# One decoder step on one core: pairwise weight sums built in SBUF tiles, with small edits at the head, the sample values, the page units and the tail

## The chip, the core and the metric

The kernel runs on one core of one Trainium2 chip, as one launch. The metric is the device time of one execution in microseconds (us), the median of several runs of the same program. The engines are named as the profile names them: PE (matrix engine; PEld are its weight loads), DVE (vector), ACT (scalar), POOL (general), SP (the queue that issues most transfers). A "q" behind a name (SPq, ACTq) is that engine's instruction queue, which takes its instructions strictly in order: an instruction that waits holds all those behind it.

## What is computed

One inference step of a single decoder layer over 512 prompt tokens and 64 sample tokens (8 sequences of 8), model width 2048. All projections come from one combined weight `w_in`:

```python
z = jnp.einsum('btd,de->bte', h, w_in)             # h = rms_norm(x, norm_in)
qa, ka, va, ga, qi, ki, wi, qb, kb, vb, gb, ab = jnp.split(z, offs, axis=-1)
...
att = dsa_prompt(qa, ka, va, qi, ki, wi)           # top-k of index scores, then softmax attention
att = dsa_sample(qa, ka, va, qi, ki, wi, cache_k, cache_v, cache_idx_k, page_table)
ob, s_fin = gla(qb, kb, vb, la, s0)                # gated linear attention, 4 heads
...
a = att.reshape(B, T, -1) * jax.nn.silu(ga)
bpart = rms_norm(o_b, gla_norm).reshape(B, T, -1).astype(a.dtype) * jax.nn.silu(gb)
xs = xs + jnp.einsum('bte,ed->btd', jnp.concatenate([a, bpart], axis=-1), w_out)
y_sample = rms_norm(xs, norm_f)
```

Eight attention heads of 128 read a paged cache of 1024 past positions for the sample tokens. The outputs are the normalised result for both token sets, and the new keys, values, index keys and linear-attention states.

## The kernel before, in words

Each float32 matrix product is made of three matmuls on rounded parts: a weight tile `w_raw` (128 x 512) is loaded by SP, ACT casts it to a rounded `w_hi` (L196), and the remainder `w_lo` is subtracted on DVE or POOL (L199). `wload` (L188) does this for one weight tile, with 3 buffers of `w_raw` and 5 of each part; `gemm` runs four such tiles per column block of 128. `WOFF` is the priority offset by which the scheduler hoists weight loads ahead of other work. `lo_eng` names the engine of the remainder: POOL during heads 0 to 3, DVE otherwise.

The program runs in stages. At the head, `split_x` (L221) loads the transposed tokens k-slice by k-slice and splits them into `xh` and `xl`, and `first_piece` (L208) splits the first weights. Then come the index projections and `sample_scores`, whose per-sequence key parts are `kch` and `kcl` (L508, L509). Heads 0 to 3 follow (`head`), with projections q and k (each rotated, then cast to `qh`, `kh` on ACT at L630), scores, the gate `ga`, and `head_out`. During them the prompt's top-k runs in the background (`turned`, `far`, `top`). `vgroup` (L649) makes the values of four heads at once; its last lines make the sample rows of the values: copy of one half of an accumulator into the tile `v_smp`, an add of the other half, a scale by the tokens' norm into `vaS`. The tile `v_smp` has the tag `e1`, that is, it shares two buffers with `v_tok`, whose contents go out by transfers.

In heads 4 to 7 and later, `units` reads the paged cache: each unit fetches tiles `kt` or `vt`, multiplies scores (`pS`, 32 output columns at a time), takes the softmax and multiplies by values. `filler` steps the units between the pieces of the gemms, one step of the generator `unit_steps` at a time.

The output projection uses a fast two-by-two scheme: besides the plain blocks of `w_out` it needs four sums of blocks (S1 = block 01 + ..., and so on), for the first half of the rows (p = 0) and for the second (p = 1). Those of p = 0 are added on DVE in tiles `bs` within `units`. Those of p = 1 live in the DRAM tile `spill_t[1]`, which rows of the trace call `st`. `block_parts` (L771) lists 16 pieces of 512 KB. In heads 0 to 2 each of the next weight loads is followed by one transfer `st<-in_wo` on SP (L194: DRAM to DRAM), 16 in all. In heads 2 and 3, each remainder on POOL is followed by one accumulating transfer on POOL's queue (L203): 8 of `st<-in_wo`, then 8 of `st<-st`, DRAM to DRAM.

At the tail the last matmuls (`acc_s`) give the sample rows of the last quarter in two pieces of 256 columns. They are folded (two partition halves of the accumulator and the residual `ysm`), squared and summed (L1584), the root and its reciprocal taken (L1449, L1587), and both halves scaled and stored (L1589 to L1592).

Of the kernel before, what the change touches and what calls it, by code (L numbers as in the profile page):

```python
# [10 lines left out]
F32 = mybir.dt.float32  # L11
# [108 lines left out]
def build(tc, I, O):  # L120
# [64 lines left out]
    started, added = [], []  # L185

    def wload(src, far=0):
        with tc.high_priority(offset=WOFF):  # L188
# [3 lines left out]
            if started:  # L192
                with tc.issue_after(wloads[-1]):
                    sy.dma_start(*started.pop(0))  # L194
# [5 lines left out]
            if lo_eng[0] is po_:  # L200
                if added:
                    with tc.issue_after(getattr(c, "ins", c)):
                        po_.dma_start(*added.pop(0), accum_op=ALU.add)  # L203
# [4 lines left out]
    def first_piece(b, k):  # L208
# [10 lines left out]
        ve.tensor_tensor(out=lo[:, c], in0=raw[:, c], in1=hi[:, c].bitcast(F32), op=ALU.subtract)  # L219

    def split_x(k):  # L221
        if k == 0:
            sy.dma_start(x0[:, : NK + HT], I["x0"][:, : NK + HT])
            sy.dma_start(x0[:, NK + HT :], I["x0"][:, NK + HT :])
            first_piece(0, k)
# [12 lines left out]
        for c, x in parts:  # L238
            ve.scalar_tensor_tensor(out=l[:, c], in0=x, scalar=gn_in[:, k : k + 1], in1=h[:, c].bitcast(F32), op0=ALU.mult, op1=ALU.subtract)
# [106 lines left out]
    po_.memset(vaS[:TS], 0.0)  # L346
# [131 lines left out]
    def sample_scores():  # L478
# [14 lines left out]
        for half in range(2):  # L493
            for grp in range(2):
                for m in range(4):
# [12 lines left out]
                    ve.tensor_tensor(out=kcl[hr], in0=raw, in1=kch[hr].bitcast(F32), op=ALU.subtract)  # L508
                    se.copy(kcl[other], kcl[hr].bitcast(F32))  # L509
# [139 lines left out]
    def vgroup(g, step):  # L649
# [48 lines left out]
        vt = ev.tile([P, 512], F32, name="v_smp", tag="e1", bufs=2)  # L698
        se.copy(vt[TS:], accs[4][:TS])
        ve.tensor_tensor(out=vt[TS:], in0=accs[4][TS:], in1=vt[TS:], op=ALU.add)  # L700
        to = vaS[TS:, cols] if g < 2 else vt[TS:]
        ve.tensor_scalar(out=to, in0=vt[TS:], scalar1=sst[TS:, 4:5], scalar2=None, op0=ALU.mult)
# [68 lines left out]
    def block_parts():  # L771
        first, second = [(0, 0), (0, 1), (1, 1), (1, 0)], [(0, 1), (1, 1), 0, 2]
        for j in range(4):
            for k in range(0, 8, 2):
                block = lambda half, q: I["wo"][2 + q, :, 8 * half + k : 8 * half + k + 2, :]
                more = block(*second[j]) if j < 2 else spill_t[1][:, second[j], k : k + 2, :]
                yield spill_t[1][:, j, k : k + 2, :], block(*first[j]), more

    def head(h, bg, n):
# [7 lines left out]
        if h == 0:  # L787
# [10 lines left out]
            for to, src, _ in block_parts():  # L798
                started.append((to, src))
        if h == 2:  # L800
            assert not started
            for to, _, more in block_parts():
                added.append((to, more))
# [869 lines left out]
```

## Time and profile before

| | us |
|---|---|
| runs | 1203.16, 1198.15, 1203.48; median 1203.16 |
| profiled execution | 1195.22 |
| its span | 1193.3 |
| granted PE clock over the span | 0.998 |
| PE busy in the span | 1179.5 (99%) |
| PEld, DVE, ACT, POOL busy | 1039.7, 727.4, 584.8, 307.2 |
| DMA over the span | 260 MB, 218 GB/s |

The span runs from the first to the last instruction that the profiler records; 1.9 us of the profiled execution lie around it. PE's busy time includes overlapping starts of pipelined matmuls, so what counts below is the time in which PE had no matmul to run: 1193.3 - 1179.5 = 13.8 us. In rows of waits, "A <- B: t, n" says that A stood idle for t us, n times, until B released it. In the chain of waits the columns are start, duration, and what filled that time.

### The profile page before, as it was taken

The page shows a single profiled execution, that of the slowest core. Times are in us where ns is not written, and L with a number is a line of the kernel's source. Part 1 is how long each engine was busy: PE and PEld are TensorE (multiplying, and loading weights), DVE is VectorE, ACT ScalarE, POOL GpSimd, SP SyncE. Part 2 cuts the span into 40 slices and gives each one's busy share as a digit, 9 for nine tenths or more (in the row PEclk, how much of TensorE's full clock was granted, in tenths as well). Part 3 has the DMA queues.
Part 4 walks back from the last instruction along what each step waited for, and adds up shares of the span by engine and source line. Part 5 has one row for each costly group of instructions (what it writes and reads, how often), then busy time and mean ns, then how long its engine had stood idle before and what let it go on. Part 6 is the DMA issues. An engine that isn't in the chain of part 4 may idle for free.

```text
span 1193.3 us, 22985 instructions
## 1 busy us (share of the span) xinstructions
PE 1179.5 (99%) x8383; PEld 1039.7 (87%) x8389; DVE 727.4 (61%) x1347; ACT 584.8 (49%) x1044; POOL 307.2 (26%) x495
## 2 busy tenths in 40 slices
PE   9999999999999999999999999999999999999997
PEld 8999987799999779789998769778899999888886
DVE  6677899699746432565445434434566444657786
ACT  6887564444443332345344435426367533544454
POOL 1225665446631110100112311321041221012100
PEclk9999999999999999999999999999999999999999
DMA  8662233876973999988867675677715377669873
GB/s 291 212 179 95 91 107 108 265 234 160 227 189 92 363 328 373 346 313 304 283 207 244 221 266 202 228 242 227 253 46 179 123 257 240 220 173 234 244 234 116
DMA packets 142419, 259.98 MB, mean 218 GB/s; under 512 B 15633, under 2 KB 38818, under 8 KB 141730
## 3 DMA queue, kind: packets, MB, share of 16 engines
q1 hardware_dynamic: 136370, 243.83, 60.9%
q0 software_dynamic: 4928, 13.11, 6.3%
q10 hardware_dynamic: 1008, 1.57, 0.4%
q8 instruction: 66, 1.08, 0.4%
q14 instruction: 47, 0.39, 0.1%
HBM read 224.62 MB, written 50.48 MB: 231 GB/s over the span
## 4 chain that ended last, share of the span: by engine, by line
PE 82%; DVE 7%; DMA 5%; issue 2%; ACT 2%; SPq 1%; POOL 1%; ACTq 0%; DVEq 0%; POOLq 0%
PE ps_g L249 37%; PE ps_g L254 6%; PE ps_g L662 5%; PE ps_g L664 5%; PE ps_g L663 5%; PE pOs L284 2%; PE acc L1390 2%; PE acc L1389 2%; PE acc L1391 2%; PE pS L284 2%; DMA w_raw<-in_w 2%; DMA y<-in_xp 2%; PE ps_v L658 1%; PE ps_v L659 1%; DVE w_lo L1384 1%
## 5 line engine op out<-in xcount | busy, mean ns | idle before, releaser
L249 PE MATMUL ps_g<-xh,w_hi 128*128 128x288 f32 x1312 | 391.6, 298 | 0.2 <-ACT xh L237 0.2
L249 PE MATMUL ps_g<-xl,w_hi 128*128 128x288 f32 x1312 | 287.6, 296 | 0.0
L249 PE MATMUL ps_g<-xh,w_lo 128*128 128x288 f32 x1312 | 284.5, 296 | 0.6 <-DVE w_lo L219 0.6
L196 ACT CAST w_hi<-w_raw 128x512 fp32r<-128x512 f32 x252 | 154.2, 619 | 250.4 <-PE ps_g L249 94.0
L249 PEld LDWEIGHTS ps_g<-xh,w_hi 128*128 128x128 f32 x1312 | 246.5, 188 | 4.7 <-issue 2.5
L199 DVE TENSOR_TENSOR w_lo<-w_raw,w_hi 128x512 fp32r<-128x512 f32 x188 | 134.9, 723 | 181.2 <-ACT w_hi L196 176.6
L249 PEld LDWEIGHTS ps_g<-xl,w_hi 128*128 128x128 f32 x1312 | 212.3, 188 | 2.3 <-issue 1.2
L249 PEld LDWEIGHTS ps_g<-xh,w_lo 128*128 128x128 f32 x1312 | 211.4, 188 | 1.6 <-DVE w_lo L219 0.8
L199 POOL TENSOR_TENSOR w_lo<-w_raw,w_hi 128x512 fp32r<-128x512 f32 x64 | 86.9, 1359 | 54.9 <-ACT w_hi L196 46.5
L662 PE MATMUL ps_g<-w_hi,xh 128*128 128x512 f32 x256 | 100.7, 395 | 0.0
L664 PE MATMUL ps_g<-w_hi,xl 128*128 128x512 f32 x256 | 100.6, 393 | 0.0
L663 PE MATMUL ps_g<-w_lo,xh 128*128 128x512 f32 x256 | 100.1, 391 | 0.0
L1384 DVE TENSOR_TENSOR w_lo<-w_raw,w_hi 128x1024 fp32r<-128x1024 f32 (+1 forms) x60 | 68.3, 1150 | 42.4 <-ACT w_hi L1382 42.2
L1382 ACT CAST w_hi<-w_raw 128x1024 fp32r<-128x1024 f32 (+1 forms) x60 | 59.4, 994 | 62.5 <-PE acc_s L1394 21.8
L1390 PE MATMUL acc<-w_lo,fh 128*128 128x512 f32 x216 | 84.1, 389 | 0.0
L1391 PE MATMUL acc<-w_hi,fl 128*128 128x512 f32 x216 | 84.1, 389 | 0.0
L1389 PE MATMUL acc<-w_hi,fh 128*128 128x512 f32 x216 | 83.6, 389 | 0.0
L664 PEld LDWEIGHTS ps_g<-w_hi,xl 128*128 128x128 f32 x256 | 48.1, 188 | 10.7 <-issue 0.8
L662 PEld LDWEIGHTS ps_g<-w_hi,xh 128*128 128x128 f32 x256 | 48.0, 188 | 10.0 <-DVE ev_t L622 0.3
L663 PEld LDWEIGHTS ps_g<-w_lo,xh 128*128 128x128 f32 x256 | 48.1, 188 | 9.7
L623 POOL TENSOR_TENSOR ev_sw<-ev_sw,c_s 128x576 f32<-128x576 f32 x16 | 25.3, 1581 | 88.3 <-ACT ev_sw L620 88.2
L1389 PEld LDWEIGHTS acc<-w_hi,fh 128*128 128x128 f32 x216 | 40.5, 188 | 8.4
(394 smaller groups left out, 2089.1 us busy)
## 6 DMA issues: line engine op xcount, KB each, us to landing
w_raw<-in_w SPq DMA_DIRECT2D x188, 256.0 KB, 3.6
kt<-in_ck SPq DMA_DIRECT2D x128, 256.0 KB, 5.1
vt<-in_cv SPq DMA_DIRECT2D x128, 256.0 KB, 5.1
w_raw<-in_wv SPq DMA_DIRECT2D x64, 256.0 KB, 3.3
w_raw<-st SPq DMA_DIRECT2D x32, 512.0 KB, 5.1
w_raw<-in_wo SPq DMA_DIRECT2D x20, 512.0 KB, 6.8
st<-in_wo SPq DMA_DIRECT2D x16, 512.0 KB, 5.0
bs<-in_wo SPq DMA_DIRECT2D x32, 256.0 KB, 5.5
```

The lines of the kernel that those rows point to most:

```text
L196: c = se.copy(hi, raw)
L199: c = lo_eng[0].tensor_tensor(out=lo, in0=raw, in1=hi.bitcast(F32), op=ALU.subtract)
L249: pe.matmul(ps[:, j, :HT], wt, xt[k][:, j * HT : (j + 1) * HT], start=(k == 0 and n in (0, 2)), stop=(k == NK - 1 and n > 3))
L254: m = pe.matmul(ps[:, 0, :TQ], wt[:, c], xt[:, P:T], start=(k == 0 and n == 0), stop=(k == NK - 1 and n == 2))
L662: pe.matmul(accs[i], xh[k][:, c], wh, start=a, stop=False)
L663: pe.matmul(accs[i], xh[k][:, c], wl, start=False, stop=False)
L664: m = pe.matmul(accs[i], xl[k][:, c], wh, start=False, stop=b)
L1382: se.copy(hi, raw)
L1384: ve.tensor_tensor(out=lo, in0=raw, in1=hi.bitcast(F32), op=ALU.subtract)
L1389: pe.matmul(acc, f[0][:, k, c], wh, start=a, stop=False)
L1390: pe.matmul(acc, f[0][:, k, c], wl, start=False, stop=False)
L1391: return pe.matmul(acc, f[1][:, k, c], wh, start=False, stop=b)
```

## The change

Six edits, in the order of the program:

1. Head: `first_piece` returns its subtraction, and for k = 0 the split `xl` on DVE is issued behind the first `w_lo`.
2. `kcl`: its subtraction and copy get a higher priority.
3. Sample values: in `vgroup` 0 and 1 the copy, add and scale are done in place in `vaS`; the tile `v_smp` is left to groups 2 and 3. The clearing of `vaS` moves into `vgroup`.
4. Sums for p = 1: `block_parts` and the two lists go; `block_moves` hangs transfers on the numbered weight loads ("slots") of heads 0 to 3. The pieces are made in four groups of four, at slots 0, 7, 14, 20. A group has an SBUF tile `bt` (128 x 4 x 2 x 512, two buffers). On SP, each of its four pieces is loaded (`bt<-in_wo`, L786) behind one slot's weight load. On POOL, each gets one accumulating transfer behind a slot's remainder: two add a block of `w_out` from DRAM, two add another piece of the same tile (`bt<-bt`, L793). On SP again, each finished piece is stored to `spill_t[1]` (`st<-bt`, L796).
5. Units: in the first four heads' units (hg == 0) two rest steps stand between the first fetch and the first scores, in place of one.
6. Tail: the two partition halves of the last residual are folded earlier over all 512 columns; each of the two pieces then needs two adds in place of three (the first) or two and a copy on ACT (the second); each 256-column piece is squared by itself, and one small DVE instruction adds the first piece's sum to `pre`.

```diff
     SUMS = ((0, 0), (0, 1), (1, 1), (1, 0))
-    started, added = [], []
+    moves, slot = ({}, {}), [None]
+
+    def move(side, lead):
+        for f in moves[side].pop(slot[0], ()):
+            with tc.issue_after(lead):
+                f()
...
-            if started:
-                with tc.issue_after(wloads[-1]):
-                    sy.dma_start(*started.pop(0))
+            move(0, wloads[-1])
...
-            if lo_eng[0] is po_:
-                if added:
-                    with tc.issue_after(getattr(c, "ins", c)):
-                        po_.dma_start(*added.pop(0), accum_op=ALU.add)
+            move(1, getattr(c, "ins", c))
+            if slot[0] is not None:
+                slot[0] += 1
...
-            ve.scalar_tensor_tensor(out=l[:, c], in0=x, scalar=gn_in[:, k : k + 1], in1=h[:, c].bitcast(F32), op0=ALU.mult, op1=ALU.subtract)
+            with tc.issue_after(lo0) if k == 0 else ExitStack():
+                ve.scalar_tensor_tensor(out=l[:, c], in0=x, scalar=gn_in[:, k : k + 1], in1=h[:, c].bitcast(F32), op0=ALU.mult, op1=ALU.subtract)
...
-                    ve.tensor_tensor(out=kcl[hr], in0=raw, in1=kch[hr].bitcast(F32), op=ALU.subtract)
-                    se.copy(kcl[other], kcl[hr].bitcast(F32))
+                    with tc.high_priority(offset=WOFF // 2):
+                        ve.tensor_tensor(out=kcl[hr], in0=raw, in1=kch[hr].bitcast(F32), op=ALU.subtract)
+                        se.copy(kcl[other], kcl[hr].bitcast(F32))
...
-        vt = ev.tile([P, 512], F32, name="v_smp", tag="e1", bufs=2)
-        se.copy(vt[TS:], accs[4][:TS])
-        ve.tensor_tensor(out=vt[TS:], in0=accs[4][TS:], in1=vt[TS:], op=ALU.add)
-        to = vaS[TS:, cols] if g < 2 else vt[TS:]
-        ve.tensor_scalar(out=to, in0=vt[TS:], scalar1=sst[TS:, 4:5], scalar2=None, op0=ALU.mult)
+        if g == 0:
+            po_.memset(vaS[:TS], 0.0)
+        to = vaS[TS:, cols] if g < 2 else ev.tile([P, 512], F32, name="v_smp", tag="e1", bufs=2)[TS:]
+        se.copy(to, accs[4][:TS])
+        ve.tensor_tensor(out=to, in0=accs[4][TS:], in1=to, op=ALU.add)
+        ve.tensor_scalar(out=to, in0=to, scalar1=sst[TS:, 4:5], scalar2=None, op0=ALU.mult)
...
+    def block_moves(pl):
...
+        for g, n in enumerate((0, 7, 14, 20)):
+            k, t = 2 * g, []
+
+            def load(t, k, j):
+                if j == 0:
+                    t.append(pl.tile([P, 4, 2, 512], F32, name="bt", bufs=2))
+                sy.dma_start(t[0][:, j], block(k, j))
...
+            def add(t, k, j):
+                po_.dma_start(t[0][:, j], block(k, j + 1) if j < 2 else t[0][:, (0, 2)[j - 2]], accum_op=ALU.add)
+
+            def keep(t, k, j):
+                sy.dma_start(spill_t[1][:, j, k : k + 2, :], t[0][:, j])
+
+            for j in range(4):
+                at(0, n + j, load, t, k, j)
+                at(1, n + (2, 3, 5, 8)[j], add, t, k, j)
+                at(0, n + (6, 7, 8, 11)[j], keep, t, k, j)
...
         if hg == 0:
-            yield
+            yield from rest(2)
...
-            if s == 0:
-                plus(t[r], a[r2], t[r2])
-                done[ve] = plus(ys, ys, t[r])
-            else:
-                with behind(done, se):
-                    se.copy(yl[r], a[r2])
-                done[ve] = plus(ys, ys, yl[r])
+            done[ve] = plus(ys, a[r2], ys)
+        jk = ev.tile([P, 512], F32, name="yjk", tag="e1", bufs=2)
+        with behind(done, se):
+            done[se] = se.activation(jk[r, :256], ys, AF.Square, accum_out=ysq[r, 4, 3 + s : 4 + s])
+    with behind(done, ve):
+        done[ve] = ve.scalar_tensor_tensor(out=pre[r, 4:5], in0=ysq[r, 4, 3:4], scalar=1.0 / D, in1=pre[r, 4:5], op0=ALU.mult, op1=ALU.add)
     with behind(done, ve):
         scaled(1, 3)
-    jk = ev.tile([P, 512], F32, name="yjk", tag="e1", bufs=2)
-    se.activation(jk[r], y_smp[r, 512:], AF.Square, accum_out=ysq[r, 4, 4:5])
```

What moves on the engines' queues is shown at three places. The first is SP's queue in head 0, behind the values of `vgroup` 0. `w_raw` are weight loads, `st` is the DRAM tile of the sums, `v` the values read back; a name behind "waits" is the semaphore on which the row waits (DMAHW: an earlier transfer of SP or ACT; DMASW: one of POOL; Pool: an instruction of POOL). Before:

```order
L190 DMA w_raw<-in_w 128x512 [waits DMAHW5_49,Pool_49]
L194 DMA st_560<-in_wo 128x1024 [waits DMAHW6_49]
L707 DMA v_3121<-sv_539 128x4x128 [waits DMAHW7_49,DMAHW0_49]
L190 DMA w_raw<-in_w 128x512 [waits Pool_49]
L194 DMA st_560<-in_wo 128x1024 [waits DMAHW1_49]
L190 DMA w_raw<-in_w 128x512 [waits DMAHW2_49,Pool_49]
L194 DMA st_560<-in_wo 128x1024 [waits DMAHW3_49]
L190 DMA w_raw<-in_w 128x512 [waits DMAHW5_49,DMAHW4_49,Pool_49]
L194 DMA st_560<-in_wo 128x1024
```

And now:

```order
L195 DMA w_raw<-in_w 128x512 [waits DMAHW1_49,Pool_49]
L786 DMA bt<-in_wo 128x1024 [waits DMAHW2_49]
L195 DMA w_raw<-in_w 128x512 [waits DMAHW4_49,DMAHW3_49,Pool_49]
L796 DMA st_560<-bt 128x1024 [waits DMASW0_49]
L712 DMA v_3366<-sv_539 128x4x128 [waits DMAHW6_49,DMAHW5_49,DVE_49]
L195 DMA w_raw<-in_w 128x512 [waits DMAHW7_49,Pool_49]
L796 DMA st_560<-bt 128x1024 [waits DMASW1_49]
L195 DMA w_raw<-in_w 128x512 [waits DMAHW1_49,DMAHW0_49,Pool_49]
L195 DMA w_raw<-in_w 128x512 [waits DMAHW3_49,Pool_49]
L796 DMA st_560<-bt 128x1024 [waits DMAHW2_49,DMASW2_49]
L796 DMA st_560<-bt 128x1024 [waits DMASW3_49]
L195 DMA w_raw<-in_w 128x512 [waits DMAHW6_49,DMAHW4_49,Pool_49]
```

Between the weight loads stood loads of pieces into DRAM, which wait only for earlier transfers; now the stores `st<-bt` stand there, and each waits for the accumulating transfer of POOL that finishes its piece. Seven loads `bt<-in_wo` stand ahead of these rows, five of them in a row.

The second place is POOL's queue, with the remainders `w_lo`, the top-k's small copies `turned` and the accumulating transfers. Before, where the first of them stand, behind the 49th remainder on POOL:

```order
L199 TENSOR_TENSOR w_lo<-w_raw,w_hi 128x512
L203 DMA st_560<-in_wo 128x1024
L623 TENSOR_TENSOR ev_sw<-ev_sw,c_s_1535 128x576
L542 COPY turned<-top 128x8
L199 TENSOR_TENSOR w_lo<-w_raw,w_hi 128x512
L203 DMA st_560<-in_wo 128x1024
L542 COPY turned<-top 128x8
L638 COPY qaS<-ev_t_3681 128x64
```

And now the first of them, behind the 38th (`gaS` is head 0's gate):

```order
L546 COPY turned<-top 128x8
L793 DMA bt<-in_wo 128x1024
L202 TENSOR_TENSOR w_lo<-w_raw,w_hi 128x512
L546 COPY turned<-top 128x8
L793 DMA bt<-in_wo 128x1024
L546 COPY turned<-top 128x8
L202 TENSOR_TENSOR w_lo<-w_raw,w_hi 128x512
L546 COPY turned<-top 128x8
L202 TENSOR_TENSOR w_lo<-w_raw,w_hi 128x512
L546 COPY turned<-top 128x8
L727 COPY gaS<-ga 128x64
L793 DMA bt<-bt 128x1024
```

The sixteen accumulating transfers stood behind the 49th to the 64th remainder; now they stand behind the 38th to the 61st, and those of `bt<-bt` among those from `in_wo`, where before all eight of `st<-in_wo` came ahead of all eight of `st<-st`.

The third place is the end of DVE's queue, from the last prompt reciprocal on. Before:

```order
L1453 RECIPROCAL yr<-yr 128x1
L1365 TENSOR_TENSOR y_smp<-acc_s,ysm_12836 64x256
L1365 TENSOR_TENSOR ysm_12836<-acc_s,ysm_12836 64x256
L1365 TENSOR_TENSOR y_smp<-y_smp,ysm_12836 64x256
L1365 TENSOR_TENSOR y_smp<-acc_s,ysm_12836 64x256
L1365 TENSOR_TENSOR y_smp<-y_smp,yl 64x256
L1458 SCALAR_TENSOR_TENSOR y_12830<-y_12830,yr,e_12152 128x512
L1587 RECIPROCAL yr<-yr 64x1 x2
L1591 SCALAR_TENSOR_TENSOR y_smp<-y_smp,yr,nfs 128x512
```

And now:

```order
L1476 RECIPROCAL yr<-yr 128x1
L1388 TENSOR_TENSOR y_smp<-acc_s,ysm_12858 64x256
L1388 TENSOR_TENSOR y_smp<-acc_s,y_smp 64x256
L1388 TENSOR_TENSOR y_smp<-acc_s,ysm_12858 64x256
L1388 TENSOR_TENSOR y_smp<-acc_s,y_smp 64x256
L1602 SCALAR_TENSOR_TENSOR pre<-ysq,pre 64x1
L1481 SCALAR_TENSOR_TENSOR y_12852<-y_12852,yr,e_12174 128x512
L1607 RECIPROCAL yr<-yr 64x1 x2
L1611 SCALAR_TENSOR_TENSOR y_smp<-y_smp,yr,nfs 128x512
```

Of the five folds on the sample rows four are left, a small instruction (L1602) stands ahead of the last prompt scale (L1458 before, L1481 now).

On DVE's queue at the head the first `w_lo` and the first `xl` change places. Around the `kcl` rows no row of DVE, ACT or PE changes its place. From head 4 on, the units' rows stand about one fill later among the gemms' rows.

More of the change, by code (lines that the diff above doesn't have):

```diff
@@ L218, in first_piece @@
         (ve.tensor_copy if k == 0 else se.copy)(hi[:, c], raw[:, c])
-        ve.tensor_tensor(out=lo[:, c], in0=raw[:, c], in1=hi[:, c].bitcast(F32), op=ALU.subtract)
+        m = ve.tensor_tensor(out=lo[:, c], in0=raw[:, c], in1=hi[:, c].bitcast(F32), op=ALU.subtract)
+        return getattr(m, "ins", m)
     def split_x(k):
@@ L224, in split_x @@
             sy.dma_start(x0[:, NK + HT :], I["x0"][:, NK + HT :])
-            first_piece(0, k)
+            lo0 = first_piece(0, k)
             parts = ((slice(HT, T), x0[:, NK : NK + HT]), (slice(0, HT), x0[:, NK + HT :]))
@@ L345, in build @@
     vaS = sm.tile([P, HA * DH], F32, name="vaS", tag="vaS")
-    po_.memset(vaS[:TS], 0.0)
     gaS = sm.tile([P, HA, TS], F32, name="gaS", tag="gaS")
@@ L769, in head_out, with at, block @@
         sy.dma_start(spill_a[h], g1[:, :TP])
[L771 to L777, printed above, removed]
+    def block_moves(pl):
+        def at(side, n, f, *args):
+            moves[side].setdefault(n, []).append(partial(f, *args))
+        for g, n in enumerate((0, 7, 14, 20)):
[4 more added lines that the diff above has]
+                sy.dma_start(t[0][:, j], block(k, j))
+            def block(k, j):
+                half, q = SUMS[j]
+                return I["wo"][2 + q, :, 8 * half + k : 8 * half + k + 2, :]
+            def add(t, k, j):
[6 more added lines that the diff above has]
+                at(0, n + (6, 7, 8, 11)[j], keep, t, k, j)
     def head(h, bg, n):
@@ L797, in head @@
             pump(bg, 3)
[L798 to L803, printed above, removed]
+            px["b"], px["bs"] = pool("bt", 2, side="right")
+            block_moves(px["b"])
+            slot[0] = 0
         Pi = head_scores(h, q, k)
@@ L976, in build @@
     lo_eng[0] = ve
-    assert not added
+    slot[0] = None
+    assert not any(moves)
+    px["bs"].close()
     with tc.issue_after(px["end"]):
@@ L1547, in build @@
     ve.scalar_tensor_tensor(out=pre[TS:, 4:5], in0=pre[TS:, 4:5], scalar=-EPS, in1=pre[TS:, 5:6], op0=ALU.add, op1=ALU.add)
-    yl = ev.tile([P, T], F32, name="yl", tag="e0", bufs=2)[:, :256]
+    yl = ev.tile([P, T], F32, name="yl", tag="e0", bufs=2)[:, :512]
     r, r2 = halves_of(3)
-    se.copy(yl[r], ysm[3][r2, 256:])
-    plus(ysm[3][r, 256:], ysm[3][r, 256:], yl[r])
+    se.copy(yl[r], ysm[3][r2])
+    plus(ysm[3][r], ysm[3][r], yl[r])
     accs = (pg.tile([P, 2, 512], F32, name="acc", tag="ps_g")[:, 0, :], pm.tile([P, 512], F32, name="acc_u", tag="pu", bufs=1))
```

## Prediction

> **What bounds the kernel now.** I read the page first, then the waits of PE, then a table of stretches for the stage that the change rebuilds, then the chain of waits around each stall. The page's busy times:
>
> ```profile
> PE 1179.5 (99%) x8383; PEld 1039.7 (87%) x8389; DVE 727.4 (61%) x1347; ACT 584.8 (49%) x1044; POOL 307.2 (26%) x495
> ```
>
> PE has a matmul to run in all but 13.8 us of the span of 1193.3 us. Nothing in this change removes a matmul, so it can only take from those 13.8 us or add to them. Part of them is out of reach: what stands before the first matmul and after the last. The waits of PE name what can be reached:
>
> ```profile
> PE pq L733 <- ACT kh L630: 1.1, 1, 1.1
> ...
> PE pacc L281 <- ACT rl L515: 0.8, 1, 0.8
> PE pq L513 <- ACT kcl L509: 0.8, 1, 0.8
> PE ps_g L249 <- DVE w_lo L219: 0.6, 1, 0.6
> PE pS L281 <- issue: 0.5, 2, 0.3
> ```
>
> Each is a single event. The change touches each of these in some way; the row left out is PE's wait before its first matmul. The largest lies in the stage of heads 0 to 3, where the sums are built, so I cut that stage into three stretches: before the accumulating transfers, while eight of them come from `in_wo`, and while eight go from `st` to `st`.
>
> ```profile
> 225.00:282.00 57.00, 56.22 (x425) 53.17 (x424) 45.19 (x113) 28.06 (x51) 22.76 (x38) 1.00 0.70 230
> 282.00:314.00 32.00, 31.78 (x237) 31.18 (x236) 31.52 (x68) 11.56 (x24) 22.42 (x35) 1.00 1.00 217
> 314.00:347.00 33.00, 31.89 (x241) 31.41 (x240) 11.15 (x23) 13.84 (x24) 19.62 (x21) 1.00 1.00 223
> ```
>
> The columns are the stretch and its length, then busy time of PE, PEld, DVE, ACT and POOL, the granted PE clock, the share of time that the DMA engines were busy, and GB/s. PE lacks 0.78, 0.22 and 1.11 us. The clock is full, so only waiting counts.
>
> **Sample values (`v_smp`).** The chain of waits at the first of these stalls:
>
> ```profile
> 226.52 6.62 DMA out_v<-v_tok
> ...
> 233.24 0.58 ACT v_smp L699
> ...
> 233.84 0.61 ACT rl L515
> ...
> 234.49 0.62 PE pacc L281
> ```
>
> ACT's copy into `v_smp` needs a buffer of the tag that `v_tok` uses, and that is free only when the transfer out has landed, 6.62 us after its issue. The relu `rl` stands behind the copy on ACT, and PE waits for `rl`. Writing into `vaS` takes the buffer out of the chain; `vaS` is cleared long before. ACT would have been free some 3 us earlier, so the whole wait of 0.8 us goes, and nothing is late in its place that the rows show. Value -0.8, between -0.8 and -0.5, the latter if the next matmuls then meet a wait of the kind of the 0.3 us issue gaps.
>
> **Sums in SBUF.** What these stalls cost, and how the transfers behave, the same three stretches show in their lists of issues (size of one, median time to landing), first 225 to 282:
>
> ```profile
> st<-in_wo SPq DMA_DIRECT2D x11, 512.0 KB, 5.0
> w_raw<-in_w SPq DMA_DIRECT2D x14, 256.0 KB, 3.2
> ```
>
> then 282 to 314:
>
> ```profile
> st<-in_wo POOLq DMA_DIRECT2D x8, 512.0 KB, 7.7
> w_raw<-in_w SPq DMA_DIRECT2D x8, 256.0 KB, 4.4
> ```
>
> then 314 to 347:
>
> ```profile
> st<-st POOLq DMA_DIRECT2D x8, 512.0 KB, 8.4
> w_raw<-in_w SPq DMA_DIRECT2D x9, 256.0 KB, 8.6
> ```
>
> A weight load beside accumulating transfers takes 4.4 us, and beside those that read and write the same DRAM tile 8.6 us. The chain of waits shows what that does, and ACT's waits for 225 to 345 what it does in all:
>
> ```profile
> 336.63 8.96 DMA w_raw<-in_w
> ...
> 345.69 0.62 ACT w_hi L196
> 346.31 0.53 ACT kh L630
> ...
> 346.88 0.33 PE pq L733
> ```
> ```profile
> ACT w_hi L196 <- DMA w_raw<-in_w: 10.1, 5, 4.2
> ```
>
> A cast waits for its slow weight, `kh` stands behind the cast, PE waits for `kh`: 1.1 us. So 10.1 us of ACT's waiting before late weights cost PE 1.1 us, or 0.11 us for each.
>
> The change takes away the eight `st<-st` and puts SBUF-to-SBUF transfers in their place, spread among the others: sixteen accumulating transfers stood behind 16 remainders in a row, and now stand behind 24. It adds 16 stores of 512 KB, and makes each wait, on SP, for an accumulating transfer. Behind a waiting store on SP stand the next weight loads, then the values `v` for the next head. The order gives the lead. Let slot 0 be the first weight tile of head 0's gate, the 33rd on POOL. The first store stands on SP behind the load of slot 11, which needs the raw buffer of slot 8 back from its remainder; its accumulating transfer stands on POOL behind the remainder of slot 5 (the 38th). That is a lead of three slots, and most later stores have two. The slots are
>
> ```profile
> L190 SPq DMA_DIRECT2D w_raw<-in_w x31: 327/328/531, 225.0 to 339.6; - x31
> ```
>
> 114.6 us / 30 = 3.8 us apart, so a lead of two slots is 7.6 us, against 7.7 and 8.4 us of landing: each of some eleven stores holds SP for 0.1 to 0.8 us, 5 us in all by the middle. SBUF-side accumulating is in the trace only elsewhere,
>
> ```profile
> y<-in_xp POOLq DMA_DIRECT2D x16, 256.0 KB, 6.7
> ```
>
> half the size in 6.7 us, so nothing says that it would be quicker than 7.7. A weight load should land between 4.4 and 8.6 us; with fewer accumulating transfers to the slot I put it near 5, an estimate from those two rows, and late weights at 2 us of ACT's time. With SP's 5 us, that makes (5 + 2) x 0.11 = 0.8 us of PE's time, in place of 1.1: -0.3. Bounds: -1.1, if no cast waits, as in 225 to 314; +4, if the landings stay at 8.6 for all 24 slots as they were for nine (24/9 x 1.1 = 2.9) and SP's hold is double on top (10 x 0.11 = 1.1), with the old 1.1 not even taken off.
>
> The Trainium skill, page "DMA: Bandwidth & Descriptors", section "Anatomy of one DMA — SWDGE (gpsimd) path", fits a transfer with 2.0 us plus bytes over 436 GB/s, by which 512 KB would land in 3.2 us, an estimate from that page. By it no store would hold SP, and this term would be -1.1. The rows above, 7.7 and 8.4 us, decide against it here.
>
> **Units.** The chain where the first scores of the units begin, and the weight queue's wait there:
>
> ```profile
> 400.66 0.30 issue
> 400.96 0.59 PE pS L281
> ```
> ```profile
> PEld pS L281 <- DMA kt<-in_ck: 0.7, 1, 0.7
> ```
>
> The first `kt` has just arrived when PE wants it. One rest step more puts a fill's worth of gemm matmuls in between; then the 0.3 us go. The whole of the units of heads 4 to 7 moves against the gemms by one fill, so a new gap of this size may open elsewhere: 0 to -0.5, taken -0.3.
>
> **Head and `kcl`.** On DVE the first `w_lo` now comes ahead of `xl`; PE waits 0.6 us for it (row above). But soon after,
>
> ```profile
> 9.00 1.51 ACT L237 ACTIVATE xh<-xr,x 128x576 fp32r<-128x576 f32 x2 [1.15 <-DMA xr<-in_xT]
> ```
> ```profile
> 9.83 0.40 PE L249 MATMUL ps_g<-xh,w_hi 128*128 128x288 f32 x1
> ```
>
> the next token slice is split when its transfer lands, its first half ends at about 9.76, and PE takes it at 9.83. Earlier matmuls would only wait there. Value 0; -0.5 if the slice should come earlier. For `kcl` the priority moves no row on any engine, so its 0.8 us stay: 0.
>
> **Tail.** The last rows, from the chain, and the last matmul and prompt scale, from the timeline:
>
> ```profile
> 1185.75 0.44 DVE y_smp L1365
> ...
> 1186.21 0.37 ACT yl L1579
> ...
> 1187.06 0.73 ACT yjk L1584 x2
> ...
> 1187.81 0.30 ACT yr L1449
> ...
> 1188.14 0.16 DVE yr L1587
> ```
> ```profile
> 1185.16 0.28 PE L1395 MATMUL acc_s<-w_lo,ms 128*128 128x256 f32 x1
> ...
> 1187.06 0.75 DVE L1458 SCALAR_TENSOR_TENSOR y<-y,yr,e 128x512 f32<-128x512 f32 x1
> ```
>
> One add less for the first piece lets the second piece's add start when its matmul ends, 1185.47, not 1185.75. The second add follows directly, without ACT's copy: it ends at 1185.47 + 2 x 0.45 = 1186.37. Squaring 256 columns I put at 0.5 (512 took 0.73): 1186.9. The root ends at 1187.2. Meanwhile DVE does the small add (0.2, an estimate from the 0.16 of `yr`) and the prompt scale, to 1186.4 + 0.2 + 0.75 = 1187.35, and the reciprocal, behind it, starts at 1187.4 instead of 1188.14. What is late next is the prompt scale. Value -0.7, between -0.4 (the first piece's square delays ACT) and -0.8.
>
> **The sum.** -0.8 - 0.3 - 0.3 + 0 + 0 - 0.7 = -2.1 us. The profiled execution would go from 1195.22 to 1193.1. It lies 7.9 us under the median of the runs; a change of single stalls shifts all alike, so the forecast is 1203.16 - 2.1 = 1201.1 us. About 0.5%, 6 us, is what a measurement of this kernel can tell from no change, so this is no change.
>
> **Rivals.** (a) *Stores hold SP; slower.* If the accumulating transfers land late, stores stop SP, weights come late, casts stop ACT, and `kh`, `qh` or the softmax behind them stop PE. For it: leads of only two slots, 16 transfers more, DMA engines already busy all the time from 282 on, and one load of `v` that took 12.3 us there. Against it: PE lost only 1.1 us in the worst 33 us. It begins to count from a landing of 7.6 us. At 12.3 us each of 16 holds is 4.7 us, 75 us in all, x 0.11 = 8.3, less 1.1 + 0.8 + 0.3 + 0.7: +5.4, 1208.6; at 13 us it passes 0.5%, at 1210. Chance 0.10 for slower by over 0.5%. The same section of the Trainium skill's page says that a wait for a semaphore is served on the issuing sequencer before the transfer is handed on, which is this mechanism; the trace agrees in SP's waits, where twelve weight loads stood 14.6 us for an earlier one to land:
>
> ```profile
> SPq L190 <- DMA w_raw<-in_w: 14.6, 12, 4.0
> ```
>
> (b) *All stalls go; still no change that can be told.* Every late weight, the head and `kcl` too: -0.8 - 1.1 - 0.5 - 0.5 - 0.8 - 0.8 = -4.5, 1198.7. No stall in the profile gives 6 us. Chance 0.15. (c) *The gain of runs.* The three runs lie 3 to 8 us above the profiled execution. If that excess is weights that come late in some executions, a calmer DMA stage takes part of it too: to 1198.15 - 2.1 = 1196.0, faster by 0.6%. The profile shows no such excess. Chance 0.20. (d) *It does not do what it says:* sums no quicker, units no better; only `v_smp` and the tail, -1.5 or with new waits 0: 1201.7 to 1203.2. Chance 0.20.
>
> **How the numbers follow.** The forecast has 0.35, (b) 0.15, (c) 0.20, (d) 0.20, (a) 0.10. Faster by over 0.5% is (c): 0.20. Slower is (a): 0.10. Within, the rest: 0.70. The range leaves out the end of (a) and half of (c): from 1195 (below the lowest run less 2.1) to 1208 (the highest run, 1203.48, plus the bound of +4, rounded).
>
> **What would show it.** Right: no wait of `pacc` for `rl` near 234; no `kh` wait of 1 us near 346; `w_raw` landings of 4.5 to 6 us through 240 to 340; the last reciprocal 0.7 us nearer to the last matmul; `kcl`'s 0.8 us unchanged. Wrong: SP waiting for `bt<-bt` by more than 10 us in all, ACT waiting over 20 us before `w_hi` for late weights, new PE waits behind ACT in heads 0 to 3, or a gap of several us in the units.

## The result, and the profile after

| | before | after |
|---|---|---|
| median of 7 runs each (those of before: the three shown above and four more) | 1194.96 us | 1209.68 us |
| lowest and highest | 1193.08, 1203.48 | 1206.46, 1215.62 |
| ratio | | 1.0116, 95% interval 1.0092 to 1.0140 |
| profiled execution | 1195.22 us | 1215.62 us |
| its span; granted PE clock | 1193.3; 0.998 | 1213.8; 0.994 |

The change makes the kernel 14.7 us slower (13.9 by the ratio). I had forecast 2.1 us less; 1209.68 lies above the range, on the other side of no change. The profiled execution is the longest of the seven after runs, so its 20.4 us overstate the loss by some 6 us.

The busy times on the page after:

```profile
PE 1186.4 (98%) x8389; PEld 1043.4 (86%) x8389; DVE 729.3 (60%) x1347; ACT 584.7 (48%) x1045; POOL 313.7 (26%) x495
```

PE had no matmul to run for 1213.8 - 1186.4 = 27.4 us, where it was 13.8: 13.6 more. And the same matmuls took 6.9 us longer, which is mostly clock, as shown below. Together that is the 20.5 us by which the span grew. The waits of PE after:

```profile
PE pq L738 <- DVE ga L772: 5.7, 1, 5.7
PE pv L769 <- ACT th L766: 3.9, 2, 2.1
PE acc L1413 <- DVE w_lo L1407: 3.1, 4, 1.3
PE ps_g L253 <- ACT ev_sw L624: 1.3, 1, 1.3
...
PE pq L517 <- ACT kcl L513: 0.7, 1, 0.7
PE pO L1252 <- DVE Sst L1261: 0.7, 1, 0.7
PE pS L285 <- issue: 0.4, 1, 0.4
PE ps_g L253 <- DVE w_lo L221: 0.2, 1, 0.2
```

Of the small waits of before, those for `rl` and `kh` are gone, those for `kcl` and at the first `pS` ("issue") are about as they were, and waits of 0.7 us for `xh` (left out here) and `Sst` are new. The four rows at the top are new as well; all but that for `w_lo` lie in heads 0 to 3, 10.9 us in all. That stage in three stretches, first after, then before (PE, PEld, DVE, ACT, POOL, then clock, DMA share and GB/s):

```profile
238.00:275.00 37.00, 33.12 (x258) 32.26 (x255) 26.24 (x69) 11.72 (x23) 16.19 (x26) 1.00 1.01 285
275.00:310.00 35.00, 30.09 (x205) 29.22 (x206) 32.58 (x71) 16.25 (x31) 21.55 (x32) 0.90 0.96 294
310.00:347.00 37.00, 34.93 (x250) 34.25 (x249) 21.80 (x48) 15.41 (x29) 18.84 (x26) 0.95 0.99 304
```
```profile
238.00:275.00 37.00, 37.00 (x290) 36.30 (x289) 34.06 (x88) 16.56 (x32) 15.67 (x26) 1.00 0.71 224
275.00:310.00 35.00, 34.78 (x261) 34.18 (x260) 34.48 (x71) 15.15 (x25) 25.11 (x38) 1.00 0.83 184
310.00:347.00 37.00, 35.88 (x271) 35.41 (x271) 15.15 (x36) 15.94 (x31) 20.35 (x22) 1.00 1.01 226
```

PE lacks 3.88, 4.91 and 2.07 us, 10.86 in all; before it lacked 1.34. That is 9.5 us of waiting. Clocks of 0.90 and 0.95 take another 0.10 x 35 + 0.05 x 37 = 5.4 us, some 0.5 us of it while PE stood idle anyway. The sum, 14.4 to 14.9, agrees with where the output stage begins. Its first matmul before and after, from the timelines:

```profile
1003.71 0.39 PE L1389 MATMUL acc<-w_hi,fh 128*128 128x512 f32 x1
```
```profile
1018.75 0.39 PE L1412 MATMUL acc<-w_hi,fh 128*128 128x512 f32 x1
```

It starts 15.0 us later, about as much as the medians differ, and nearly all of that is lost in these 109 us. (The other 5 us of the profiled execution come in the output stage, most of it with the 3.1 us for `w_lo`; that wait is between 0 and 3.1 us in the profiles of the kernels below, with and without the loss.)

The DMA share is what changed ahead of all else: before, the engines were at 0.71 and 0.83 and full only in the last stretch; after, they are full from 238 on. The issues of 238 to 275 after (size, median time to landing):

```profile
bt<-in_wo SPq DMA_DIRECT2D x8, 512.0 KB, 6.8
bt<-in_wo POOLq DMA_DIRECT2D x4, 512.0 KB, 9.4
st<-bt SPq DMA_DIRECT2D x4, 512.0 KB, 12.6
w_raw<-in_w SPq DMA_DIRECT2D x7, 256.0 KB, 11.5
...
v<-sv SPq DMA_DIRECT2D x2, 256.0 KB, 14.0
```

A weight load takes 11.5 us in this stretch, where it took 2.9 before; I had put it near 5. Over all of 238 to 350 the median is 6.3 us (before 3.6) and the longest 18.4 (before 11.8). The chain of waits shows what follows:

```profile
245.45 11.79 DMA w_raw<-in_w
...
259.35 15.13 DMA w_raw<-in_w
...
274.58 0.62 ACT w_hi L199
...
277.99 0.61 DVE ga L772
...
278.64 0.80 PE pq L738
...
280.51 7.01 PE ps_g L253 x41
...
287.63 0.93 PE ps_g L253 x7
```

The weight comes 15 us after its issue. Its cast stands ahead of the softmax `p` (L748) on ACT's queue; DVE's steps of the softmax wait for that, `ga` stands behind them, and PE waits 5.7 us for `ga`. Then the clock: the next 41 matmuls take 171 ns each, later ones of the same line 133 ns. The same happens once more at 333, by way of `th`:

```profile
315.57 17.08 DMA w_raw<-in_w
...
333.39 0.59 ACT th L766
...
334.02 0.50 PE pv L769
```

### The profile page after: what moved, and what is told of

It is laid out like the page before. It is cut to its first block, busy times and chain, and to the rows that moved or that the text cites. A ratio compares the mean times of both kernels' runs of the same rounds, so it can differ in the third digit from the quotient of the medians.

```text
span 1213.8 us, 23044 instructions
## 1 busy us (share of the span) xinstructions
PE 1186.4 (98%) x8389; PEld 1043.4 (86%) x8389; DVE 729.3 (60%) x1347; ACT 584.7 (48%) x1045; POOL 313.7 (26%) x495
## 4 chain that ended last, share of the span: by engine, by line
PE 78%; DMA 10%; DVE 6%; issue 2%; ACT 2%; POOL 1%; SPq 1%; ACTq 0%; DVEq 0%; POOLq 0%
PE ps_g L253 35%; PE ps_g L258 6%; PE ps_g L666 5%; PE ps_g L668 5%; PE ps_g L667 5%; DMA w_raw<-in_w 4%; DMA y<-in_xp 2%; PE acc L1412 2%; PE acc L1413 2%; PE acc L1414 2%; PE pS L288 2%; PE pOs L288 2%; PE ps_v L662 1%; DVE w_lo L1407 1%; PE ps_v L663 1%
## 5 line engine op out<-in xcount | busy, mean ns | idle before, releaser
L1413 PEld LDWEIGHTS acc<-w_lo,fh 128*128 128x128 f32 x216 | 40.5, 188 | 13.0 <-DVE w_lo L1407 4.8
```

The costliest lines, as they stand in the source:

```text
L1413: pe.matmul(acc, f[0][:, k, c], wl, start=False, stop=False)
```

## The experiments

The theory was that the DMA engines have more work in this stage than they can do in it, so that everything that SP issues lands late, whichever queue it is in. Its rivals: that a store which waits for its accumulating transfer holds SP (rival a of the prediction); that the 16 loads and 16 stores lie in front of the weights in SP's own line of transfers; that the early start, five loads in a row, is to blame; that only the place of the casts on ACT's queue is; and that another of the six edits makes the loss.

| kernel | ratio to before, 95% | DMA share 238 to 347 | PE idle there, us |
|---|---|---|---|
| before | 1 | 0.85 | 1.3 |
| after | 1.0116 (1.0092 to 1.0140) | 0.99 | 10.9 |
| sums alone | 1.0125 (1.0103 to 1.0148) | 0.98 | 13.0 |
| all but the sums | 1.0001 (0.9985 to 1.0017) | 0.84 | 1.5 |
| loads issued by ACT | 1.0122 (1.0095 to 1.0149) | 0.98 | 10.1 |
| no stores | 1.0050 (1.0034 to 1.0067) | 0.90 | 3.3 |
| no accumulating transfers | 0.9999 (0.9984 to 1.0014) | 0.72 | 0.0 |
| plain transfers in their place | 1.0031 (1.0015 to 1.0047) | 0.88 | 3.9 |
| before, with 16 spare copies | 1.0063 (1.0041 to 1.0085) | 0.96 | 2.3 |
| later and closer moves | 1.0102 (1.0074 to 1.0130) | 0.93 | 7.4 |
| five `w_raw` buffers | 1.0101 (1.0073 to 1.0130) | 1.00 | 4.8 |

The share and PE's idle time are each kernel's row of a windows table for 238 to 347 in one profiled execution. The kernels below are edits of the changed one unless "before" is named.

**Sums alone, and all but the sums.** The first is before with edit 4 only, the second is after without it:

```diff
-    started, added = [], []
+    moves, slot = ({}, {}), [None]
...
-    def block_parts():
...
+    def block_moves(pl):
```

> The kernel before with the SBUF sums alone. If the sums carry the loss, as the trace says (PE loses 14 us between 240 and 366 us of the profiled execution), it comes out 12 to 16 us above the kernel before, ratio 1.010 to 1.014, with the v_smp wait of 0.8 us still there. If a part of the loss belongs to the tail, the units or the sample values (the trace of the change also lost 4 us in the output stage), it is 8 to 10 us above, ratio 1.007 to 1.009.

> The change without the SBUF sums (block sums in DRAM as before). By the prediction's other terms, -0.8 (sample values), -0.3 (units), -0.7 (tail), it is 1.8 us under the kernel before, ratio 0.9985; the wait of kh for a late weight near 346 stays. If the output stage's 4 us belong to the tail's edit, it is 2 us above, ratio 1.002.

Sums alone: 1212.55 against 1195.24 us, 14.9 us by the ratio: all of the loss. PE's longest wait in it is that of after:

```profile
PE pq L735 <- DVE ga L769: 5.7, 1, 5.7
```

All but the sums: 1195.61, no difference, where 0.9985 was expected. So the other five edits neither make the loss nor bring a gain that can be told.

**Loads issued by ACT.** The 16 loads `bt<-in_wo` leave SP's queue:

```diff
-                sy.dma_start(t[0][:, j], block(k, j))
+                se.dma_start(t[0][:, j], block(k, j))
```

> The change with the sixteen loads of pieces issued by ACT's queue, so that they stand in another ring than the weights. Theory A (weights wait behind bursts in SP's own ring): weight loads of 240 to 270 us land in 5 to 9 us instead of 10 to 15, the first stall of PE (5.7 us) goes, and the kernel is 4 to 8 us above the kernel before. Theory B (the DMA engines have too much to move, whichever ring): landings stay above 10 us and the time within 2 us of the change, 14 us above. Theory C (SP is held by waiting stores): as B, since the stores stay on SP.

1211.06 us: no relief. The queue list of 225 to 370 shows that the loads did move, to q10 (packets, MB, share of the engines):

```profile
q10 hardware_dynamic: 2304, 8.39, 15.4%
```

Yet PE waited 7.3 us for `ga`, and weight loads still took 11.2 us in 238 to 275. So the loads in SP's own line are not what holds the weights. The Trainium skill, page "DMA: Bandwidth & Descriptors", section "Issuing engines are not separate DMA queues", says that transfers of all issuing engines end up on the same 16 DMA engines and interleave there. The trace agrees: 1.0122 with the loads on the other queue, 1.0116 without.

**No stores, and no accumulating transfers.** Each leaves out one kind of move:

```diff
-                at(0, n + (6, 7, 8, 11)[j], keep, t, k, j)
...
+        if p == 1:
+            return I["wo"][2 * p + 1, :, k : k + n, :]
```
```diff
-                at(1, n + (2, 3, 5, 8)[j], add, t, k, j)
```

> The change without the sixteen stores of finished pieces; the output stage reads plain blocks of w_out in their place, so this leaves out the sums' way into the result. Theory A: the first burst (five loads in a row) stays, so the first stall of 5.7 us stays, the second near 320 goes: 5 to 9 us above the kernel before. Theory B: 8 MB of 39 go, DMA share falls from 1.0 to 0.85, nearly all of the loss goes: 0 to 4 us above. Theory C: nothing holds SP, all goes, 0 to 2 us above, and SP's waits show it.

> The change without the sixteen accumulating transfers, so the pieces stored are single blocks and not sums. Theory B (the stage asks more of the DMA engines than they move): a third of their busy time goes, weight loads land under 8 us, and 0 to 5 us above the kernel before, as without the stores (+6.7) or better. Theory D (it is the stores' and loads' own queue on SP): the loss stays at 8 us or more.

Without the stores nearly half of the loss stays (1201.95), though nothing is left on SP that waits for an accumulating transfer. So rival (a)'s way is at most a part. But my theory missed too: it gave 0 to 4 us, and 6.0 to 6.7 is what the rival of the early burst gave. I come back to this below. SP's waits of after for 225 to 370 speak against rival (a) more strongly:

```profile
SPq L572 <- DMA st<-bt: 3.1, 2, 3.0
...
SPq L796 <- DMA sa<-ga: 1.1, 1, 1.1
...
SPq L796 <- DMA bt<-in_wo: 0.6, 1, 0.6
...
SPq L796 <- DMA w_raw<-in_w: 0.5, 1, 0.5
```

L796 are the stores: they were held 2.2 us in these three rows, and two small copies (`far<-turned`, L572) waited 3.1 us for a store to land. Against that stand the 75 us of rival (a). Without the accumulating transfers, but with the 16 stores and 16 loads, nothing is lost (1194.97). ACT's waits of 238 to 350 in that kernel:

```profile
ACT w_hi L199 <- DMA w_raw<-in_w: 3.1, 3, 1.5
```

Before has 15.7 us there in six waits, the longest 5.6; after has 26.5 us in nine, the longest 9.2.

**Plain transfers in place of the accumulating ones.** POOL still issues 16 transfers of 512 KB into `bt`, at the same places, but they don't add:

```diff
-                po_.dma_start(t[0][:, j], block(k, j + 1) if j < 2 else t[0][:, (0, 2)[j - 2]], accum_op=ALU.add)
+                po_.dma_start(t[0][:, j], block(k, (j + 1) % 4))
```

> The change with each accumulating transfer replaced by a plain load of the same 512 KB into the same tile by the same queue, so the pieces stored are single blocks and not sums. If the number of transfers and of SP's waiting stores makes the loss, it stays at 10 us or more. If the engines' time does (a packet of 4096 bytes of an accumulating transfer takes 327 ns in the trace, a plain one 159), half of the 42 us goes, and the loss is 0 to 4 us.

1201.28 against 1196.85: 3.7 to 4.4 us instead of 14.7, at the upper end of what was expected. The queue of POOL (q0) in 225 to 370, in this kernel, and both large queues in after and before, tell why:

```profile
q0 software_dynamic: 2304, 8.39, 16.9%
```
```profile
q1 hardware_dynamic: 13968, 30.74, 59.1%
q0 software_dynamic: 2304, 8.39, 30.1%
```
```profile
q1 hardware_dynamic: 11575, 21.12, 44.7%
q0 software_dynamic: 2304, 8.39, 32.3%
```

The same 8.39 MB in the same 2304 packets take 16.9% of the engines' time as plain transfers and 30.1% as accumulating ones. Before, from DRAM to DRAM, they took 32.3%. So working in SBUF saves 2.2% of 145 us, 3.2 us of engine time, while the stores and loads on q1 cost 14.4%, 20.9 us. What is left of the loss here is not traced to a late transfer: PE waits 3.5 us for `ga` (L724), behind an unbroken run of top-k and softmax work on DVE.

The sum of engine time is not the whole story, though. The two queues took 77.0% before and 89.2% after; without the stores they took 77.4% (46.7 and 30.7), and with plain transfers 76.1% (59.2 and 16.9). So in this window these two kernels ask no more of the engines than before, which had five of its 16 first moves behind it by then, and still lose 0.50% and 0.31%. What differs is where the work lies: without the stores the share is 1.01, 0.99 and 0.71 in the three stretches, before it was 0.71, 0.83 and 1.01. Nor does a full share stall PE by itself: without the accumulating transfers the first stretch stands at 0.97 and PE lacks nothing; with plain ones it stands at 1.01, as in after, but the engines move 374 GB/s there instead of 285, a weight load takes 7.4 us instead of 11.5, and PE lacks 0.41 us instead of 3.88. So weights come late where the engines get more than they serve at that time, and accumulating transfers, which take more engine time, bring that about sooner.

**Before, with 16 spare copies.** The other way round: the kernel before, with 16 copies of 512 KB inside DRAM, one behind every second weight load from head 0 on:

```diff
+            if extra:
+                turn[0] += 1
+                if turn[0] % 2 == 0:
+                    with tc.issue_after(wloads[-1]):
+                        sy.dma_start(*extra.pop(0))
```

> The kernel before with sixteen more plain copies of 512 KB from DRAM to a spare DRAM tile, one behind every second weight load from head 0 on; nothing reads them. If any extra work for the DMA engines in this stage makes weights late (their share is 0.70 before 282 us and 1.00 from there to 347), the kernel becomes 3 to 10 us slower, with weight loads near 300 us landing above 8 us. If it is the SBUF tiles, the store waits or their place that cost, it is at most 1.5 us slower.

1204.44 against 1196.85: slower by 0.63%, without one instruction of the change. The weight loads of 238 to 350 in this kernel, then in the one before:

```profile
w_raw<-in_w SPq DMA_DIRECT2D x29, 256.0 KB, 6.2
```
```profile
w_raw<-in_w SPq DMA_DIRECT2D x30, 256.0 KB, 3.6
```

Near 300 I had expected over 8 us: for 282 to 347 the median is 8.1 us, but in before it is 7.7 there. ACT's waits before `w_hi` for 238 to 350 go from 15.7 to 22.5 us. Nothing waits for the copies' result; they only use the engines and a place in SP's line, which the loads on ACT's queue showed not to matter for the 16 loads. So added engine time makes a loss of this kind by itself, though this one is half as large.

**Later and closer moves.** The groups start at slots 8, 13, 18, 22, so that the five loads in a row are gone, and adds and stores follow their loads sooner:

```diff
-        for g, n in enumerate((0, 7, 14, 20)):
+        for g, n in enumerate((8, 13, 18, 22)):
...
-                at(1, n + (2, 3, 5, 8)[j], add, t, k, j)
-                at(0, n + (6, 7, 8, 11)[j], keep, t, k, j)
+                at(1, n + (2, 3, 4, 6)[j], add, t, k, j)
+                at(0, n + (4, 5, 6, 8)[j], keep, t, k, j)
```

> The change with the four groups at slots 8, 13, 18, 22 and the steps of a group closer together, so that loads do not pile up when the tile pool opens, but the same bytes fall into 23 slots instead of 31. If the pile of five loads at 238 us is the cause, the first stall goes and the loss is 0 to 6 us. If the sum of bytes is (theory B), 1.36 MB per slot of 3.8 us would need about 358 GB/s, more than the 300 seen, so weights stay late over the whole stretch and the loss is 14 us or more.

1207.75 us, 1.0102, 12.3 us above before: far from the 0 to 6 us by which the early burst would be the cause, and not quite the 14 of the theory. The three stretches:

```profile
238.00:275.00 37.00, 37.00 (x277) 36.46 (x276) 35.70 (x93) 16.82 (x33) 17.66 (x29) 1.00 0.79 230
275.00:310.00 35.00, 33.24 (x246) 32.31 (x246) 29.58 (x61) 12.21 (x22) 22.08 (x33) 1.00 1.04 310
310.00:347.00 37.00, 31.32 (x215) 30.43 (x214) 14.62 (x33) 14.43 (x28) 15.23 (x18) 0.91 0.98 286
```

The first stretch has no stall any more and a share of 0.79; the loss has gone to the later ones, where the same bytes now crowd into 23 slots instead of 31. The burst of loads at 238 is one such crowd, and without it there is another. A kernel that starts these moves earlier or spreads them wider was not run, so how much of the loss a better place would save is open.

**Casts on POOL.** If the order on ACT alone were to blame, moving the casts of this stage away from ACT would free the softmax:

```diff
-            c = se.copy(hi, raw)
+            c = po_.tensor_copy(hi, raw) if slot[0] is not None else se.copy(hi, raw)
```

> The change with the casts w_hi of heads 0 to 3 on POOL instead of ACT; the transfers are the same. Theory E (late weights hurt because ACT, held at a cast, cannot do the softmax and the other casts that PE needs): weight loads still land 10 to 17 us late, but PE's stall of 5.7 us behind the softmax goes, and the loss falls from 14 to 5 us or less. Theory F (PE simply runs out of weights): PE now waits for w_lo or w_hi themselves, and the loss stays at 10 us or more. POOL's own work behind its casts (top-k copies, rotation) may add 1 to 3 us in both.

1221.59 against 1195.43, ratio 1.0211 (1.0171 to 1.0251), the slowest of all. PE's first wait:

```profile
PE ps_g L253 <- POOL w_lo L202: 10.0, 4, 4.7
```

POOL now waits for the late weights and does the casts and the remainders one after the other, so the gemms themselves run dry. It doesn't tell the order on ACT from the late weights, since it adds work to POOL; it shows that the lateness reaches PE by another engine too.

**Five buffers of `w_raw`.** More loads ahead, paid for with one `w_hi` and one `w_lo` fewer, in the changed kernel and, for the price of the buffers, in the one before:

```diff
-            raw = wp.tile([P, 512], F32, name="w_raw", tag="w_raw", bufs=3)
+            raw = wp.tile([P, 512], F32, name="w_raw", tag="w_raw", bufs=5)
...
-            hi = wp.tile([P, 512], F32R, name="w_hi", tag="w_hi", bufs=5)
+            hi = wp.tile([P, 512], F32R, name="w_hi", tag="w_hi", bufs=4)
...
-            lo = low_tile(wp, 5, far)
+            lo = low_tile(wp, 4, far)
```

> The change with five raw weight buffers instead of three, and four instead of five of each split part (the same SBUF space). A weight load then has 5 x 3.8 = 19 us before its cast is due, more than the 10 to 17 us in which the late ones land. If lateness against the cast is what costs (theories B and E together), ACT's waits for weights fall from 29 us to under 10 and the loss from 14 to 5 us or less. If fewer split parts make PE wait, or the longer queue only moves the delay to other loads, it stays at 10 us or more.

> The kernel before with five raw weight buffers and four of each split part. If that size alone costs nothing (within 1 us of the kernel before), the 10 to 12 us that the change with five raw buffers still loses are all its transfers'. If it is 3 us or more slower, as the kcl wait of 2.3 us in that trace hints, so much of the loss there belongs to the buffers.

1207.06 against 1195.43 with the change; 1199.5 against 1196.85 without (1.0020, 1.0005 to 1.0035), so the buffers by themselves cost 2.4 to 2.7 us, between the two cases expected; PE's wait for `kcl` is 2.3 us in both kernels with five buffers and 0.7 or 0.8 in all others. ACT's waits before `w_hi` for 238 to 350 fall from 26.5 to 2.1 us, and the longest wait goes from `ga` to the values. The chain there:

```profile
242.53 17.64 DMA v<-sv
...
260.19 0.63 ACT vh L717
...
260.86 0.79 PE pv L769
```

`v` is issued behind the weights that now run ahead, and takes 17.64 us. The loss stays at 11.6 to 12.1 us, though hardly a cast waits any more: with the engines still full (share 1.00), the transfer that is late and stalls PE is another one.

**Values and tail alone.** Before, with edits 3 and 6, the two from which I had expected 1.5 us:

```diff
-        vt = ev.tile([P, 512], F32, name="v_smp", tag="e1", bufs=2)
...
+        to = vaS[TS:, cols] if g < 2 else ev.tile([P, 512], F32, name="v_smp", tag="e1", bufs=2)[TS:]
...
+            done[ve] = plus(ys, a[r2], ys)
```

> The kernel before with the sample values' and the tail's edits alone. By the prediction 0.8 and 0.7 us faster, ratio 0.9987; against the change without the sums (ratio 1.0001) this tells whether the units' extra rest step takes back the gain: then the linear-attention wait of 0.6 to 1.1 us (pO for Sst) that every kernel with that step shows is not in this trace. If it is there, or the ratio is 1.000 or more, the tail's gain is given back elsewhere.

1195.04 against 1196.85, ratio 0.9997 (0.9984 to 1.0010): the medians are 1.8 us apart, but the ratio tells no change, and a gain of 1.5 us, 0.13%, lies just inside its interval. The wait at `pO` for `Sst` is not in this profile. A small wait stands in this profile that before hadn't:

```profile
PE pS L281 <- DMA kt<-in_ck: 1.4, 1, 1.4
```

## Why the prediction was wrong, point by point

**What bounds the kernel.** Right as far as it went: PE, with 13.8 us of idle time. What I did not draw from it is the other side. Nothing could gain more than a few us, but nothing limits a loss.

**The sums.** Here the prediction failed, at three points of one term: -0.3 us was forecast for it, and the sums alone came out 14.9 us slower.

First, "with fewer accumulating transfers to the slot I put it near 5". That took a landing time as a property of the transfer and its neighbours. Here it was mostly a wait in line: the share of the engines in the rows of 225 to 347, 0.70 and then 1.00, stood in front of me, and I did not add up the engine time that the change brings. It could be done from before's rows. A `st<-st` went, but as many accumulating transfers came, and the price of those in SBUF was the unknown; at an unchanged 32.3% of 145 us and 16 more stores at the rate of q1 (44.7% for 21.12 MB, so 8.39 MB are 18% of 145 us, 26 us, an estimate), the stage of 109 us at 0.85 has to take 26 us with only 16 free. Measured were 20.9 us more on q1. The work that doesn't fit becomes lateness: 11.5 us in place of 5 in the first stretch, and up to 18.4 us singly.

Second, "0.11 us for each" us of ACT's waiting. None of the five waits in that row reached PE. The one that did, 5.6 us long, ends at 345.7, just behind the window of 225 to 345; with it there were 15.7 us in six waits. A mean rate is also the wrong form. Before, 5.6 us cost PE 1.1, and 4.2 us cost nothing; after, 9.2 us cost 5.7, and 4.9 us in two waits near 332 cost 2.1; with ACT's loads, 9.4 cost 7.3. So between 2 and 4.5 us of a wait were hidden, and what was longer reached PE. Without the stores, 2.4 us reached PE behind two waits of 5.0 and 1.6 us that end at 252.3 and 256.5, the second for `v`: waits close together seem to add up. These are few events, and what sets the hidden part is not shown.

Third, the clock was taken as full throughout. Behind the stalls it was not, and that cost about 5 us of the 15.

The upper bound of +4 took "the landings stay at 8.6" as the worst case, with that same mean rate; both were too low: the first stretch had 11.5.

**Rival (a)**, with chance 0.10, had the sign and the last links right (late weights, casts that stop ACT, the softmax behind them, PE), and a time of 1208.6 close to what came. The time is luck: it is 5.4 us on top of a median of 1203.16, and what came is 14.7 us on top of 1194.96. Its cause was wrong: the stores hardly waited, and without them nearly half of the loss stays. Its condition, a landing beyond 7.6 us for the accumulating transfers, was met (9.4) for another reason. Of the signs that were to show the prediction wrong, two came: ACT waited over 20 us before `w_hi` (26.5 for 238 to 350, where before had 15.7), and PE has new waits behind ACT in heads 0 to 3. SP waiting over 10 us for `bt<-bt` did not come.

**Rival (c)**, that the median would fall with a calmer DMA stage, fell with its premise: seven runs of before have a median of 1194.96, next to the profiled 1195.22. The three first runs stood 3 to 10 us above the four later ones of the same kernel, and my 1201.1 carried that.

**`v_smp`.** Right: the wait of `pacc` for `rl` is gone.

**Units.** The gap did not go: PE's issue gap at the first scores is 0.37 us after, where it was 0.30. It is gone in all but the sums, and 0.6 in three other kernels with the step. A wait at `pO` for `Sst` has come on top, 0.7 us after. It is in all nine kernels with the step (0.2 to 1.1 us), but also in two of those without it (1.1 with the spare copies, 0.8 with five buffers in the kernel before), so what sets it is open. The gain of 0.3 us wasn't seen.

**Head and `kcl`.** Right: PE's wait for the first `w_lo` fell from 0.6 to 0.2 us, and PE then waited 0.7 us at 10.4 for the next slice `xh`, for which it had not waited before; 0.7 us for `kcl` stayed.

**Tail.** The end of after's chain:

```profile
1205.24 0.16 DVE yr L1476
...
1207.52 0.75 DVE y L1481
1208.31 0.16 DVE yr L1607
```

From the last prompt reciprocal to the sample's it is 3.07 us, before it was 1188.14 - 1184.19 = 3.95: 0.9 us less, and the prompt scale is what is late next, as forecast. The sign that I had named, the last reciprocal nearer to the last matmul, came only in values and tail alone (2.09 us behind its start, before 2.98). After it is 3.79 us: there the last prompt reciprocal comes 0.72 us behind that start instead of 0.97 ahead of it, so DVE begins the folds late. All but the sums shows the same: the last matmul starts at 1185.12, before at 1185.16, but the last prompt reciprocal at 1185.30, before at 1184.19. That takes back the gain of 0.9 us there; why DVE's prompt rows come later is open. The spans are 1194.2 us in all but the sums and 1193.3 both in values and tail alone and before, so the 0.8 us of `v_smp` were given back too, and where is not traced.

## What to carry to other kernels

Before moving bytes into a stage, add up the DMA engines' time in that stage: the share that they have, plus what the change adds by rates from the same trace, with accumulating transfers at their own rate. Do it stretch by stretch: a stage whose sum fits can still be crowded at its start. Where the work comes close to a stretch's length, expect landings to grow and the transfer with the least slack to stall its reader; here neither another queue (1.0122) nor later and closer moves (1.0102) nor more buffers (1.0101) saved much. And don't turn many small hidden waits into a price per us: look up how much the longest one hides, and price what is longer by itself, with the clock behind it.

## What the runs showed of the hardware

An accumulating transfer cost the engines 1.8 times a plain one of the same bytes and packets (30.1% against 16.9%), and the same in SBUF as in DRAM within a tenth (30.1% against 32.3%). Half of the accumulating ones in after read SBUF and half DRAM, the plain ones all DRAM, but packets of 4096 bytes take the same in both: the median of POOL's is 327 ns in after and before and 159 ns with plain transfers.

A short stall slows the matmuls behind it. Without the stores, after one wait of 2.4 us that ends near 258, two stretches of 5 us:

```profile
255.00:260.00 5.00, 2.64 (x16) 2.07 (x15) 2.86 (x6) 2.57 (x5) 3.38 (x6) 0.92 1.07 385
260.00:265.00 5.00, 5.00 (x30) 5.00 (x29) 4.83 (x12) 1.14 (x3) 3.44 (x8) 0.74 1.08 254
```

PE was busy all of the second with 30 matmuls, where the next 5 us had 41: 0.08 x 5 + 0.26 x 5 = 1.7 us of clock on top of 2.4 of waiting. In stretches of 1 us the clock is 0.50 at its lowest, here and wherever else a stall brings it down. The Trainium skill, page "TensorE: Matmul & The Clock Gate", section "Part 1: The HAM clock gate (the "warmup" mystery)", has the clock fall to half after an idle window of about 3.4 us and come back after as long a busy one. The 5.7 us stall of after agrees: the clock is 0.50 from 279 to 283. But here 2.4 us were enough, so by the measurement shorter stalls count too. Nine stalls of 2.1 to 3.5 us in these profiles brought the clock down, and each cost 1.7 us behind it; two of 2.3 and 2.4 us (with five buffers at 151, in sums alone at 258) cost nothing, so length alone doesn't decide. Waits of 1.1 us, as before's for `kh`, and up to 1.9 us (with ACT's loads) left the clock at 1.00.
